# The last part of a two-part transformer kernel: its last 256 features in two groups, the closing norm's factor by feature on ScalarE, the store by two k-tiles, and other places of tiles in SBUF

## The chip, the cores and the metric

The kernel runs on one NeuronCore of a Trainium2 chip. The metric is the time of one execution on the device in microseconds. The change is measured against the kernel before, in runs on one chip.

## The reference, cut to what matters

256 tokens of 1024 features go through two models, one behind the other, each two layers deep. The first has a context of 256 tokens beside them in its first layer; the second is called `second_block` here. All of it is fp32.

```python
def first_block(x, c, ctx, ...):
    for l in range(2):
        # h = modulate(rms_norm(x)), the same for ctx; local and grouped attention, merged with gates
        x = x + g1 * branch_merge(ya, yb, ga, gb, w_pa[l], w_pb[l], w_o[l])
        # ctx likewise where l is 0
        h2 = modulate(rms_norm(x, norm2[l]), sh2, sc2)
        x = x + g2 * swiglu(h2, w_ffn_in[l], w_ffn_out[l])
    return rms_norm(x, final_norm)

def swiglu_2(h, w_gu, w_down):                      # w_gu: 1024 x 5632, w_down: 2816 x 1024
    g, u = jnp.split(h @ w_gu, 2, axis=-1)
    return (jax.nn.silu(g) * u) @ w_down

def second_block(x, ...):
    for l in range(2):
        x = x + 0.5 * swiglu_2(rmsnorm(x, g_ffn1[l]), w_ffn1_gu[l], w_ffn1_down[l])
        x = x + hybrid_mixer(rmsnorm(x, g_mix[l]), w_in[l], ...)
        x = x + 0.5 * swiglu_2(rmsnorm(x, g_ffn2[l]), w_ffn2_gu[l], w_ffn2_down[l])
    return rmsnorm(x, g_final)                      # x / sqrt(mean(x*x) + eps) * g_final
```

## The kernel before

Features lie on the 128 partitions, tokens along the free dimension: `x` is 128 x 8 x 256, and a "k-tile" is 128 features of it. Every matmul that counts is done as three: an fp32 operand is split into a high part, rounded to TensorE's fp32r, and a low part, the rest. For a weight, `Weights.next` loads raw pieces of up to 128 x 1024 by SP (`wf_1r` and the like), and for each 128 x 512 of them ScalarE writes the high half (`hw*`, L403) and VectorE the low half (`lw*`, L408, raw minus high); eight buffers of each go round. `group` (L427 issues its matmuls) takes for each k the pairs high weight with high input, high weight with low input and low weight with high input. The weight is the stationary operand, 128 x 128; the input is the moving one, 256 tokens wide, or 512 in layer 0 of the first part, where the context goes along.

The inputs' names: `hh`, `hl` are the high and low part of a normed x in the first part (`inputs_of`, 8 k-tiles, each 516 columns wide, so that neighbouring k-tiles lie 2064 bytes apart); `gh`, `gl` the same in the second part; `acth`, `actl` the gated activations of a feed-forward; `yh`, `mh` and their `l` those of attention and of the mixer's merge. `wb` are weights of the first part's layers, `wf` those of a feed-forward (ffn2) and `wmx` of a mixer in the second part.

The tiles' places in SBUF follow from the pools' order and the tiles' sizes. In the built program, within a partition and modulo 256 bytes: raw, high and low weights 128; `gh`, `gl` and `x` 224; `act`, `yh`, `mh`, `sg`, `rt` 0; `hh` and `hl` 32 + 16k and 160 + 16k in layer 0, 0 + 16k and 128 + 16k in layer 1's feed-forward, for k-tile k.

The order on each engine is set by a scheduler that lists instructions by a modelled time, with some held back by hand: `MIX_HOLD` is the number of low weight halves that may go ahead of a mixer's last `gl` on VectorE (`L408 gl<-hn`, the low part of the mixer's normed input), and `HOLD` does the like for the row factors.

A feed-forward of the second part, `ffn2`, has 22 groups of gate/up, and then `add_x` for the down projection, four groups of 256 features with 22 k-tiles each, i.e. 132 matmuls of 256 columns. After a group, VectorE multiplies the two 128-feature halves of the result by the row factor of the norm ahead of it (`rt`, L1258) and adds that to x (L1262); ScalarE squares it (L478), VectorE adds the squares' two halves (L483), TensorE transposes them (L486) and VectorE reduces over the features into a column of `sums` (L488). After the last group, `rstd_rows` makes the row factor: mean (L504 to L509), an integer start and three Newton steps (L522 to L536), two transposes that spread it over the partitions (L542), a copy to SBUF on ScalarE (L550, `rsb`). `store` multiplies each k-tile by the feature's factor `gfin` and by that row factor (L1767, eight times 128 x 256), and SP stores four k-tiles at a time (L1771).

## Time and profile before

| what | value |
|---|---|
| time, median of 3 runs (lowest to highest) | 2473.17 us (2472.64 to 2473.49) |
| the profiled execution's own time | 2474.45 us |
| its span | 2472.6 us |
| TensorE busy | 2404.3 us (97%) |
| VectorE, ScalarE busy | 1821.5 us (74%), 1357.2 us (55%) |
| mean granted clock of TensorE | 0.988 |

The span is the time between the first and the last instruction of that execution; its own time also has what lies around. Busy times are per engine and overlap. Matmuls are pipelined: the length that the trace gives for one reaches into the next, so what one costs is read from start to start, or from the length of a piece of the chain of waits and the number of matmuls in it.

### The profile page before, as it was taken

Reading aid. Unit: us, or ns where it says so; the run is one execution under the profiler, and the core shown is the slowest. Engines: PE = TensorE matmul, PEld = TensorE weight load, DVE = VectorE, ACT = ScalarE, POOL = GpSimd, SP = SyncE. Lnnn points to the kernel's source line nnn. Section 1 sums busy time; section 2 is a strip of 40 time slices with the busy share of each in tenths; the row PEclk is TensorE's granted clock in tenths of the full one; section 3 lists DMA queues with packets and bytes.
Section 4 is the critical chain, followed back from the end, with each engine's and each line's share of the span. In section 5 each row is a group of like instructions: output and inputs, shape, how many; then the busy total and the mean of one; then the engine's idle time right before and its main releaser. Section 6 shows DMA issues by size and latency. Waiting matters only on the chain.

```text
span 2472.6 us, 45747 instructions
## 1 busy us (share of the span) xinstructions
PE 2404.3 (97%) x17232; PEld 2243.4 (91%) x17232; DVE 1821.5 (74%) x4115; ACT 1357.2 (55%) x2666; POOL 0.2 (0%) x4
## 2 busy tenths in 40 slices
PE   7999999999999999999999999999999999999997
PEld 4877779888888898999999998999999999899997
DVE  5777667885766888776676688886666669888665
ACT  4566544322223676665555567765555556776553
POOL 0000000000000000000000000000000000000000
PEclk9999999999999999999999999999999999899999
DMA  7221462553653333465555553455555555345553
GB/s 276 85 73 52 160 232 95 171 188 131 218 184 119 129 112 115 146 187 183 184 182 181 182 183 117 138 173 184 177 186 187 178 184 183 106 135 188 180 179 103
DMA packets 112542, 393.45 MB, mean 159 GB/s; under 512 B 12480, under 2 KB 13760, under 8 KB 111808
## 3 DMA queue, kind: packets, MB, share of 16 engines
q1 hardware_dynamic: 112320, 390.52, 48.8%
q8 instruction: 136, 2.23, 0.4%
q14 instruction: 86, 0.70, 0.1%
HBM read 389.42 MB, written 1.05 MB: 158 GB/s over the span
## 4 chain that ended last, share of the span: by engine, by line
PE 91%; DVE 5%; ACT 2%; issue 1%; DMA 1%; SPq 0%; DVEq 0%; ACTq 0%
PE mm L427 82%; PE y L427 2%; PE s L427 1%; PE s L798 1%; PE mm L616 1%; PE y L805 1%; DVE lwmx L408 1%; PE s L751 1%; PE y L486 0%; DMA wm0r<-in_wm_dram 0%; DVE kl L408 0%; ACT pt L775 0%; ACT hwmx L403 0%; PE y L682 0%; DVE ptl L408 0%
## 5 line engine op out<-in xcount | busy, mean ns | idle before, releaser
L427 PE MATMUL mm<-hh,hwb 128*128 128x512 f32 (+2 forms) x1176 | 349.1, 341 | 3.1 <-ACT gt L1027 1.6
L427 PE MATMUL mm<-hl,hwb 128*128 128x512 f32 (+1 forms) x1176 | 350.0, 340 | 0.2 <-DVE hl L408 0.2
L427 PE MATMUL mm<-hh,lwb 128*128 128x512 f32 (+2 forms) x1176 | 346.7, 340 | 0.0
L403 ACT ACTIVATE hwb<-wb_0r 128x512 fp32r<-128x512 f32 (+1 forms) x250 | 149.9, 612 | 261.4 <-PE mm L427 242.4
L427 PE MATMUL mm<-gh,hwf 128*128 128x256 f32 x1344 | 272.1, 283 | 0.0
L427 PE MATMUL mm<-gh,lwf 128*128 128x256 f32 x1344 | 270.7, 282 | 0.0
L427 PE MATMUL mm<-gl,hwf 128*128 128x256 f32 x1344 | 270.6, 282 | 0.0
L408 DVE TENSOR_TENSOR lwf<-wf_1r,hwf 128x512 fp32r<-128x512 f32 (+1 forms) x272 | 183.8, 676 | 110.2 <-ACT hwf L403 103.9
L408 DVE TENSOR_TENSOR lwf<-wf_0r,hwf 128x512 fp32r<-128x512 f32 (+1 forms) x272 | 183.6, 676 | 103.4 <-ACT hwf L403 96.7
L403 ACT ACTIVATE hwf<-wf_1r 128x512 fp32r<-128x512 f32 (+1 forms) x272 | 168.2, 619 | 166.6 <-PE mm L427 153.7
L403 ACT ACTIVATE hwf<-wf_0r 128x512 fp32r<-128x512 f32 (+1 forms) x272 | 168.2, 619 | 165.3 <-PE mm L427 149.4
L427 PEld LDWEIGHTS mm<-hh,hwb 128*128 128x128 f32 x1176 | 203.7, 189 | 30.3 <-ACT gt L1027 2.7
L408 DVE TENSOR_TENSOR lwb<-wb_0r,hwb 128x512 fp32r<-128x512 f32 (+1 forms) x250 | 163.6, 666 | 89.5 <-ACT hwb L403 85.5
L427 PEld LDWEIGHTS mm<-hl,hwb 128*128 128x128 f32 x1176 | 204.5, 189 | 25.8 <-DVE hl L408 0.8
L427 PEld LDWEIGHTS mm<-hh,lwb 128*128 128x128 f32 x1176 | 203.9, 189 | 25.4
L403 ACT ACTIVATE hwb<-wb_1r 128x512 fp32r<-128x512 f32 (+1 forms) x242 | 146.6, 612 | 117.6 <-PE mm L427 107.3
L427 PEld LDWEIGHTS mm<-gh,hwf 128*128 128x128 f32 x1344 | 207.5, 189 | 0.0
L427 PEld LDWEIGHTS mm<-gh,lwf 128*128 128x128 f32 x1344 | 206.7, 188 | 0.0
L408 DVE TENSOR_TENSOR lwb<-wb_1r,hwb 128x512 fp32r<-128x512 f32 (+1 forms) x242 | 158.5, 667 | 65.2 <-ACT hwb L403 62.5
L427 PEld LDWEIGHTS mm<-gl,hwf 128*128 128x128 f32 x1344 | 205.8, 188 | 0.0
L427 PE MATMUL mm<-gh,hwmx 128*128 128x256 f32 x656 | 140.5, 288 | 4.6 <-DVE kl L408 2.1
L427 PE MATMUL mm<-actl,hwf 128*128 128x256 f32 x704 | 142.0, 283 | 0.0
(393 smaller groups left out, 5558.8 us busy)
## 6 DMA issues: line engine op xcount, KB each, us to landing
wf_0r<-in_wf_dram SPq DMA_DIRECT2D x120, 512.0 KB, 3.5
wf_1r<-in_wf_dram SPq DMA_DIRECT2D x120, 512.0 KB, 3.6
wb_0r<-in_wb_dram SPq DMA_DIRECT2D x108, 512.0 KB, 3.8
wb_1r<-in_wb_dram SPq DMA_DIRECT2D x105, 512.0 KB, 3.7
wmx_0r<-in_wmx_dram SPq DMA_DIRECT2D x49, 512.0 KB, 3.6
wmx_1r<-in_wmx_dram SPq DMA_DIRECT2D x49, 512.0 KB, 3.6
wm2r<-in_wm_dram SPq DMA_DIRECT2D x48, 512.0 KB, 3.6
wm1r<-in_wm_dram SPq DMA_DIRECT2D x24, 512.0 KB, 4.7
```

What stands on the lines that cost most here:

```text
L403: self.nc.scalar.activation(out, src, AF.Copy, scale=scale)
L408: return self.nc.vector.tensor_tensor(out, src, h, ALU.subtract)
L427: i = nc.tensor.matmul(out, lhsT, rhs, start=bank not in first, stop=n[bank] == 0, skip_group_check=True)
L616: nc.tensor.matmul(ps[32 * j : 32 * j + 32], self.scp[:, k], t[:, o : o + 512], start=k < 4, stop=k >= 4, skip_group_check=True,)
L751: nc.tensor.matmul(out, q, part, start=n == 0, stop=n == 1, skip_group_check=True)
L798: nc.tensor.matmul(s[:, :nk], q[:, o], part, start=n == 0, stop=n == 1, skip_group_check=True)
L805: nc.tensor.transpose(tp[:, j * P : (j + 1) * P], pt[:, j * P : (j + 1) * P], self.ident)
```

## The change

The last feed-forward of the second part (`wf2_1`) gets its last 256 features as two groups of 128. For this `add_x` is replaced there by `last_x`: five groups (three of two k-tiles, two of one), and for a single k-tile a new `square_sum` that squares 256 columns and transposes these, with no halves to add. `sums` has five columns there. `last_x` also lets ScalarE multiply x by `gfin`, one k-tile at a time and in place, right behind its squares. `store` then has only the row factor left: four products of two k-tiles each, and a store behind each.

Elsewhere: `MIX_HOLD` goes from 5 to 6. `inputs_of` makes k-tiles 512 columns wide (520 for layer 1's feed-forward), and `qg`, `four` and `one` become wider tiles of which the same columns are used. In the built program the weights' tiles then lie at 160 modulo 256 bytes, and `act`, `yh`, `mh`, `sg`, `rt` and layer 0's `hh` and `hl` at 224, where `gh`, `gl` and `x` stay; layer 1's feed-forward has `hh` and `hl` at 224 + 32k. The number of matmuls and of raw loads is the same.

```diff
--- before.py
+++ after.py
@@ -109,9 +109,12 @@
 GQ_ROWS = [r for i in range(4) for h in (i, 4 + i) for r in _r(HD * h, HD)]
 
 
-def spec_ffn2(gu, down):
+def spec_ffn2(gu, down, last=False):
     s = [(gu, _r(128 * m, 128) + _r(DFF + 128 * m, 128), (8,)) for m in range(22)]
-    return s + [(down, _r(256 * j, 256), KP_DOWN) for j in range(4)]
+    cols = [_r(256 * j, 256) for j in range(4)]
+    if last:
+        cols[3:] = _r(768, 128), _r(896, 128)
+    return s + [(down, c, KP_DOWN) for c in cols]
 
 
 QA, KA, VA, FA, QB, KB, VB, QC, CKV, QI, KI, WI, GT = (
@@ -133,7 +136,7 @@
 
 
 
-MIX_HOLD = 5
+MIX_HOLD = 6
 MIX_ORDER = (
     "K S0 G8 T0 T1 F0 s0 S2 s1 S1 G1 G9 s3 G10 F1 s2 s4 x0 B3 G5 x2 G4 x1 d1 F2 x3 d0 G2 G0 G11 x4 x5 d2 d3 B1 G7 G3 d4 d5 A0 B2".split()
 )
@@ -188,7 +191,7 @@
     SPECS[f"wb1_{_l}"] = (_l, spec_b1(_l))
     SPECS[f"wf1_{_l}"] = (_l, spec_ffn2("w_ffn1_gu_2", "w_ffn1_down_2"))
     SPECS[f"wmx_{_l}"] = (_l, spec_mix())
-    SPECS[f"wf2_{_l}"] = (_l, spec_ffn2("w_ffn2_gu_2", "w_ffn2_down_2"))
+    SPECS[f"wf2_{_l}"] = (_l, spec_ffn2("w_ffn2_gu_2", "w_ffn2_down_2", _l == 1))
 
 
 def pieces(n, kparts):
@@ -487,6 +491,16 @@
         self.hold(0, i, hold)
         nc.vector.tensor_reduce(ss[:, j], ps[:, :SEQ].rearrange("p (t f) -> p t f", t=2), AX.X, ALU.add)
 
+    def square_sum(self, x, ss, m, j, pool):
+
+        nc = self.nc
+        sq = pool.tile([P, 2, SEQ], F32, tag="sq", name=self.u("sq"), bufs=2)[:, 0]
+        nc.scalar.activation(sq, x[:, m], AF.Square)
+        ps = self.bank("y")
+        for t in range(2):
+            nc.tensor.transpose(ps[:, t * P : (t + 1) * P], sq[:, t * P : (t + 1) * P], self.ident)
+        nc.vector.tensor_reduce(ss[:, j], ps[:, :SEQ].rearrange("p (t f) -> p t f", t=2), AX.X, ALU.add)
+
     def sums(self):
         return self.small(8, tag="sums").rearrange("p (j t) -> p j t", j=4)
 
@@ -500,8 +514,8 @@
         nc = self.nc
         p, v = self.small(2), self.small(2)
         t = ss.rearrange("p j t -> p t j")
-        if last == 3:
-            nc.vector.tensor_reduce(p, t[:, :, :3], AX.X, ALU.add)
+        if last >= 3:
+            nc.vector.tensor_reduce(p, t[:, :, :last], AX.X, ALU.add)
         else:
             nc.vector.tensor_reduce(p, t[:, :, 2:], AX.X, ALU.add)
             nc.vector.tensor_tensor(p, p, ss[:, 0], ALU.add)
@@ -576,9 +590,9 @@
             self.hi(hh[:, k : k + 2, c], t)
             self.last_norm = self.lo(hl[:, k : k + 2, c], t, hh[:, k : k + 2, c])
 
-    def inputs_of(self, pool):
-
-        return [pool.tile([P, NKT, 516], F32R, tag=f"h{c}", name=self.u(f"h{c}")) for c in "hl"]
+    def inputs_of(self, pool, n=2 * SEQ):
+
+        return [pool.tile([P, NKT, n], F32R, tag=f"h{c}", name=self.u(f"h{c}")) for c in "hl"]
 
 
     def setup_mod(self):
@@ -599,7 +613,7 @@
         self.scp = pool.tile([P, NKT, 32], F32, name="scp")
         nc.vector.memset(self.scp, 0.0)
         nc.vector.tensor_copy(self.scp[:, :, :2], self.sc)
-        self.four = pool.tile([P, 2], F32, name="four")
+        self.four = pool.tile([P, 64], F32, name="four")[:, :2]
         nc.vector.tensor_tensor(self.four, self.ident[:, 0:2], self.ident[:, 32:34], ALU.add)
         for j in (64, 96):
             nc.vector.tensor_tensor(self.four, self.four, self.ident[:, j : j + 2], ALU.add)
@@ -848,7 +862,7 @@
                         m = self.b1_merge(1, w, y[0], gates, mr.enter_context(self.open("mr1", "right")), T)
                 self.tc.keep_in_program_order(nc.scalar.preload_act_table_set("silu_and_others"))
                 self.amplitude(l, 1, len(self.xs))
-                h = self.inputs_of(hn)
+                h = self.inputs_of(hn, 520 if l else 2 * SEQ)
                 self.residual(
                     l, w, range(NKT), m, T, 16, hn, lambda i: self.norm_mod(l, 1, i, self.xs[i], h, hn, self.rsb[i]),
                     early=(lambda k: self.unnormed(l, k, h)) if l else None, place="ac"[l],
@@ -956,7 +970,7 @@
         full = lambda k: (hh[:, k, :512], hl[:, k, :512])
         mine = lambda k: (hh[:, k, :T], hl[:, k, :T])
         nt = T // P
-        qg = self.small(1, tag="qg", bufs=1)
+        qg = self.sp.tile([P, 64], F32, tag="qg", name=self.u("qg"), bufs=1)[:, :1]
         nc.vector.tensor_scalar(qg, self.p(f"qg{l}"), HD**-0.5, None, ALU.mult)
         bias_tile = lambda: ap.tile([P, 2, SEQ], F32, tag="bias", name=self.u("bias"), bufs=2)
         rot = bias_tile()
@@ -1265,6 +1279,32 @@
                 self.gained(gain, self.x, range(2 * j, 2 * j + 2))
         self.rsb = [self.rstd_rows(ss, hold=hold)]
 
+    def last_x(self, w, ks, xs, pool, rsb, scale):
+
+
+        nc = self.nc
+        ss = self.small(10, tag="sums").rearrange("p (j t) -> p j t", j=5)
+        for j, (m, n) in enumerate(((0, 2), (2, 2), (4, 2), (6, 1), (7, 1))):
+            if n == 2:
+                _, (b,) = self.pair(w.next(), ks, xs, SEQ)
+            else:
+                b = self.bank("mm")
+                self.group([(0, b[:, :SEQ], 0, P, None)], w.next(), ks, xs)
+            t = pool.tile([P, 2, SEQ], F32, tag="rt", name=self.u("rt"), bufs=2)[:, :n]
+            xv = self.x[:, m : m + n]
+            nc.vector.scalar_tensor_tensor(
+                t, b[:, : n * SEQ].rearrange("p (k t) -> p k t", k=n), scale,
+                rsb.unsqueeze(1).broadcast_to((P, n, SEQ)), ALU.mult, ALU.mult,
+            )
+            nc.vector.tensor_tensor(xv, xv, t, ALU.add)
+            if n == 2:
+                self.square_sums(self.x, ss, j, pool)
+            else:
+                self.square_sum(self.x, ss, m, j, pool)
+            for k in range(m, m + n):
+                nc.scalar.activation(self.x[:, k], self.x[:, k], AF.Copy, scale=self.p("gfin", k, 1))
+        self.rsb = [self.rstd_rows(ss, 4)]
+
     def ffn2(self, name, gain, late=None):
         nc = self.nc
         w = Weights(self, name)
@@ -1285,7 +1325,10 @@
                 acts += [(h[:, j], lo[:, j]) for j in range(2)]
                 if late and m > 2:
                     next(late, None)
-            self.add_x(w, range(22), lambda k: acts[k], fp, rsb, 0.5, gain, name[:3])
+            if gain is None:
+                self.last_x(w, range(22), lambda k: acts[k], fp, rsb, 0.5)
+            else:
+                self.add_x(w, range(22), lambda k: acts[k], fp, rsb, 0.5, gain, name[:3])
         assert w.off == w.ap.shape[0] and w.i == len(w.spec)
 
     def mixer(self, l):
@@ -1758,17 +1801,15 @@
             self.rsb = [self.rstd_rows(ss)]
 
     def setup2(self):
-        self.one = self.cp.tile([P, 1], F32, name="one")
+        self.one = self.cp.tile([P, 9], F32, name="one")[:, :1]
         self.nc.vector.memset(self.one, 1.0)
 
     def store(self, out):
         nc = self.nc
-        for k in range(NKT):
-            nc.vector.scalar_tensor_tensor(
-                self.x[:, k], self.x[:, k], self.p("gfin", k, 1), self.rsb[0], ALU.mult, ALU.mult
-            )
-            if k % 4 == 3:
-                nc.sync.dma_start(out[:, k - 3 : k + 1], self.x[:, k - 3 : k + 1])
+        for k in range(0, NKT, 2):
+            xv = self.x[:, k : k + 2]
+            nc.vector.tensor_tensor(xv, xv, self.rsb[0].unsqueeze(1).broadcast_to((P, 2, SEQ)), ALU.mult)
+            nc.sync.dma_start(out[:, k : k + 2], xv)
 
 
 def program(tc, ins, out, stages=("b10", "b11", "b20", "b21", "end"), dump=None):
```

What the scheduler makes of it, at two places. In a mixer (layer 1's is shown; `lwmx_7_2` is the low half of a weight for the values' projection, `vs` are scaled values, `hn` the normed input), VectorE has before:

```order
L408 TENSOR_TENSOR lwmx_7_0_17068<-wmx_0r_17065,hwmx_7_0_17067 128x512
L408 TENSOR_TENSOR gl_15786<-hn_16901,gh_15785 128x512
L409 SCALAR_TENSOR_TENSOR vs_16699<-mm_16835,rcol_16417,vs_16699 128x5x64
L409 SCALAR_TENSOR_TENSOR vs_16699<-mm_16836,rcol_16417,vs_16699 128x5x64
L408 TENSOR_TENSOR gl_15786<-hn_16906,gh_15785 128x512
L408 TENSOR_TENSOR lwmx_7_2_17072<-wmx_0r_17065,hwmx_7_2_17071 128x512
L408 TENSOR_TENSOR lwmx_7_4_17078<-wmx_0r_17075,hwmx_7_4_17077 128x512
L408 TENSOR_TENSOR lwmx_7_6_17082<-wmx_0r_17075,hwmx_7_6_17081 128x512
```

and now:

```order
L412 TENSOR_TENSOR lwmx_7_0_17068<-wmx_0r_17065,hwmx_7_0_17067 128x512
L412 TENSOR_TENSOR gl_15786<-hn_16901,gh_15785 128x512
L412 TENSOR_TENSOR lwmx_7_2_17072<-wmx_0r_17065,hwmx_7_2_17071 128x512
L413 SCALAR_TENSOR_TENSOR vs_16699<-mm_16835,rcol_16417,vs_16699 128x5x64
L413 SCALAR_TENSOR_TENSOR vs_16699<-mm_16836,rcol_16417,vs_16699 128x5x64
L412 TENSOR_TENSOR gl_15786<-hn_16906,gh_15785 128x512
L412 TENSOR_TENSOR lwmx_7_4_17078<-wmx_0r_17075,hwmx_7_4_17077 128x512
L412 TENSOR_TENSOR lwmx_7_6_17082<-wmx_0r_17075,hwmx_7_6_17081 128x512
```

`lwmx_7_2` has moved from behind the last `gl<-hn` to ahead of the two `vs` and of that `gl`. On TensorE the order moves too: in both mixers, and at the end of layer 1's attention in the first part, where transposes of `pt` and score matmuls stand earlier than before.

At the end of the program, VectorE has before (from the last group's scaling on):

```order
L504 TENSOR_REDUCE small_30677<-sums_29864 128x2
L508 TENSOR_SCALAR small_30677<-small_30677 128x2
L1258 SCALAR_TENSOR_TENSOR rt_30667<-mm_30534,rsb_28218 128x512
L1262 TENSOR_TENSOR x_3790<-x_3790,rt_30667 128x512
L483 TENSOR_TENSOR sq_30670<-sq_30670 128x256
L488 TENSOR_REDUCE sums_29864<-y_30673 128x2
L509 SCALAR_TENSOR_TENSOR small_30678<-sums_29864,small_30677 128x2
L522 TENSOR_SCALAR rcol_30682<-small_30678 128x2
```

and now (from the first 128-feature group's scaling on):

```order
L1295 SCALAR_TENSOR_TENSOR rt_30577<-mm_30480,rsb_28218 128x256
L1299 TENSOR_TENSOR x_3790<-x_3790,rt_30577 128x256
L502 TENSOR_REDUCE sums_29864<-y_30582 128x2
L518 TENSOR_REDUCE small_30694<-sums_29864 128x2
L522 TENSOR_SCALAR small_30694<-small_30694 128x2
L1295 SCALAR_TENSOR_TENSOR rt_30684<-mm_30587,rsb_28218 128x256
L1299 TENSOR_TENSOR x_3790<-x_3790,rt_30684 128x256
L502 TENSOR_REDUCE sums_29864<-y_30689 128x2
L523 SCALAR_TENSOR_TENSOR small_30695<-sums_29864,small_30694 128x2
L536 TENSOR_SCALAR rcol_30699<-small_30695 128x2
```

The addition of the squares' halves (L483 before) is gone for these groups, and the one scaling, addition and reduction of the last group have become two of half the width.

ScalarE has at the same place before:

```order
L403 ACTIVATE hwf_1_26_17_30520<-wf_1r_30514 128x512
L403 ACTIVATE hwf_1_26_19_30526<-wf_1r_30524 128x512
L403 ACTIVATE hwf_1_26_21_30530<-wf_1r_30524 128x256
L478 ACTIVATE sq_30670<-x_3790 128x512
L550 COPY rsb_30702<-y_30699 128x256
```

and now:

```order
L407 ACTIVATE hwf_1_27_19_30614<-wf_1r_30608 128x384
L498 ACTIVATE sq_30580<-x_3790 128x256
L1305 ACTIVATE x_3790<-x_3790,par 128x256
L498 ACTIVATE sq_30687<-x_3790 128x256
L1305 ACTIVATE x_3790<-x_3790,par 128x256
L564 COPY rsb_30719<-y_30716 128x256
```

The products with `gfin` (L1305) now stand behind each square.

## Rows read from the trace of the kernel before

**Rows 1.** The page: busy time and its share by engine; then the chain's shares.

```profile
PE 2404.3 (97%) x17232; PEld 2243.4 (91%) x17232; DVE 1821.5 (74%) x4115; ACT 1357.2 (55%) x2666; POOL 0.2 (0%) x4
...
PE 91%; DVE 5%; ACT 2%; issue 1%; DMA 1%; SPq 0%; DVEq 0%; ACTq 0%
```

**Rows 2.** Groups by shape: count, then total busy us, mean ns, idle before.

```profile
L427 PE MATMUL mm<-gh,hwf 128*128 128x256 f32 x1344 | 272.1, 283 | 0.0
...
L427 PE MATMUL mm<-hh,hwb 128*128 128x512 f32 x592 | 228.9, 398 | 1.6 <-ACT hh L403 0.9 <-ACT gt L1027 0.7
...
L408 DVE TENSOR_TENSOR lwf<-wf_1r,hwf 128x512 fp32r<-128x512 f32 x256 | 177.1, 692 | 105.7 <-ACT hwf L403 99.4 <-PE mm L427 2.9
...
L427 PE MATMUL mm<-actl,hwf 128*128 128x256 f32 x704 | 142.0, 283 | 0.0
...
L427 PE MATMUL mm<-gh,hwmx 128*128 128x256 f32 x656 | 140.5, 288 | 4.6 <-DVE kl L408 2.1 <-ACT fw L1395 1.7 <-DVE gate L1548 0.8
...
L427 PE MATMUL mm<-acth,hwb 128*128 128x256 f32 x260 | 53.2, 285 | 0.0
```

**Rows 3.** The chain in four stretches: start us, length us, line and count.

```profile
1079.96 100.04 PE mm L427 x848
...
2289.99 100.08 PE mm L427 x834
...
2417.41 15.67 PE mm L427 x132
...
534.81 56.94 PE mm L427 x245
```

**Rows 4.** Windows: busy us (instructions) of PE, PEld, DVE, ACT, POOL; PEclk, DMA.

```profile
2290.00:2390.00 100.00, 100.00 (x835) 100.00 (x835) 66.45 (x114) 55.75 (x96) 0.00 (x0) 1.00 0.58 184
1520.00:1530.00 10.00, 6.45 (x42) 5.77 (x40) 9.79 (x32) 6.64 (x15) 0.00 (x0) 0.88 0.35 112
1530.00:1540.00 10.00, 9.24 (x50) 8.68 (x49) 9.01 (x25) 6.87 (x17) 0.00 (x0) 0.60 0.01 2
```

**Rows 5.** Timeline of PE at 1103 us: start us, length us, operation, count.

```profile
1103.16 0.39 PE L427 MATMUL mm<-hl,hwb 128*128 128x256 f32 x2
1103.39 0.40 PE L427 MATMUL mm<-hh,lwb 128*128 128x256 f32 x2
...
1103.86 0.41 PE L427 MATMUL mm<-hl,hwb 128*128 128x256 f32 x2
1104.10 0.40 PE L427 MATMUL mm<-hh,lwb 128*128 128x256 f32 x2
```

**Rows 6.** The chain behind the last matmul.

```profile
2458.95 0.70 DVE rt L1258
...
2459.68 0.70 DVE x L1262
...
2460.40 0.64 ACT sq L478
...
2461.06 0.44 DVE sq L483
```

**Rows 7.** Timeline of DVE at 24.71 us, and of all engines at the end.

```profile
24.71 2.49 DVE L1743 TENSOR_TENSOR xin<-xin,rsb 128x512 f32<-128x512 f32 x4
...
2465.18 0.37 ACT L550 COPY rsb<-y 128x256 f32<-128x256 f32 x1 [4.15 <-PE y L542]
2465.59 3.25 DVE L1767 SCALAR_TENSOR_TENSOR x<-x,par,rsb 128x256 f32<-128x256 f32 x8 [1.12 <-ACT rsb L550]
```

**Rows 8.** By line and tile: count, then min, median and max ns.

```profile
L1281 DVE TENSOR_TENSOR sg<-mm,rsb x84: 413/425/427, 1255.1 to 2395.6; 128x256 f32<-128x256 f32 x84
...
L482 ACT ACTIVATE sq<-x,par x8: 492/498/501, 1191.8 to 1240.5; 128x256 f32<-128x256 f32 x8
```

**Rows 9.** The store's line: issue in ns, and time from issue to landing.

```profile
L1771 SPq DMA_DIRECT2D out_dram<-x x2: 344/346/348, 2467.3 to 2468.9; - x2
...
DMA to landing us min/median/max: 2.6/2.6/2.6
```

**Rows 10.** Timeline of PE in layer 0's mixer, idle time before and its releaser.

```profile
1525.78 0.56 PE L1689 MATMUL s<-ph,stickr 128*128 128x256 f32 x3 [2.57 <-ACT ph L403]
```

## The prediction

> **What bounds the kernel now.** I read the page first: TensorE is busy 97% of the span and the chain that ended last runs through it for 91% [rows 1]. So a microsecond is saved either where TensorE streams without a gap, by making one matmul shorter, or at the very end, where it has nothing left to do. The groups of matmuls come next [rows 2]. Each product of fp32 operands is three matmuls (high by high, high by low, low by high), and the reader is to see the counts: 1344 for each of the three products on gh and gl in the second part's gate/up, 656 in its mixers, 704 on act in its down projections, 592 of 512 columns on hh and hl in the first part's layer 0. The mean durations there (283 to 398 ns) overlap; the pitch, start to start, is what counts, and the chain gives it as a piece's length by its count.
>
> Four such pieces [rows 3], without a gap in them (the second also as a window: TensorE busy for all of 100 us at full clock [rows 4]): 100.04 us for 848, or 117.97 ns each, for the first part's feed-forward in layer 1; 100.08 us for 834, or 120.0 ns, for the last feed-forward's gate/up; 15.67 us for 132, or 118.7 ns, for its down projection; and 56.94 us for 245 of 512 columns, or 232.4 ns. The first three do the same work: 128x128 stationary, 256 columns moving, no waits. They differ by where their tiles lie in a partition, modulo 256 bytes. Stationary tiles (hw, lw) lie at 128 everywhere. The moving ones lie at 224 (gh, gl: 96 above), at 0 (act, 128 above), and in layer 1's hh and hl at a place that steps by 16 bytes with each k, so all sixteen differences come up, once for each of the 8 k on hl (0 to 112) and twice on hh (128 to 240, since hh meets hw and lw). That stage's mean is 117.97. The differences 96 and 128, taken alone, cost 120.0 and 118.7, both above that mean; so others must lie below it. In one feature group of that stage, the two hl matmuls of k=4 (difference 64) begin at 1103.16 and the next pair at 1103.39: 0.23 us; those of k=5 (80) take from 1103.86 to 1104.10: 0.24 [rows 5]. That is 115 against 120 ns, each read to 5 ns at worst, the same sign as the argument from the means.
>
> **The change, part by part.**
> *Places.* `inputs_of` loses its 4 pad columns, `qg` and `four` get 64 wide, `one` 9 wide. In the built programs the stationary tiles move to 160 and nearly all moving ones (act, mh, yh, layer 0's hh and hl) to 224, where gh and gl already were: the difference becomes 64. Layer 1's feed-forward steps by 32 bytes, and I leave it at its mean, nothing gained or lost. No run of before has a whole stage at 64, so its cost is bounded: below by the 115 ns of the pair, above by what the same tiles cost today. I take 116.5, halfway between that 115 and the mean of 117.97, since the pair is read coarsely but the means demand something below 117.97.
> - gh, gl: 3 x (1344 + 656) = 6000 [rows 2] x (120.0 - 116.5 = 3.5 ns) = 21.0 us.
> - act, 3 x (704 + 260) = 2892, in the second part's down projections and in the first part's of layer 1 [rows 2], both at place 0: x (118.7 - 116.5 = 2.2 ns) = 6.4 us. Smaller groups at that place (mh, yh) I leave out.
> - 512 columns: 3 x 592 = 1776. They go through all steps of 16 now, so only the gain from mean to best counts, and per matmul I take it as in the 256-column case: 1.5 ns, 232.4 to 230.9. 1776 x 1.5 = 2.7 us.
> Together 30.1 us. What stands outside full streams gives nothing back; TensorE carries 91% of the chain as a whole and all of it in the stages named, except the mixers, so I keep 0.95 of it: 28.6. Bounds: at 115 ns for all, 6000 x 5 + 2892 x 3.7 + 1776 x 3 = 46.0 us, at 0.95 43.7; at 117.5, 6000 x 2.5 + 2892 x 1.2 + 1776 x 0.5 = 19.4, or 18.4; the other side is in the rivals below.
>
> *The end.* Today, after the last matmul, the chain is [rows 6]: scale by the row factor 0.70, add 0.70, square on ScalarE 0.64, the two halves added 0.44, two transposes, reduction, mean and Newton steps, two transposes of the factor, a copy, then the eight products of the store. Afterwards the last group has 128 features, so these are 256 wide instead of 512. From 256-wide rows of the same kind [rows 8]: a product with the row factor 0.425 (-0.27), the add, taken like it (0.42, -0.27), the square 0.50 (-0.14); the halves' add and its step go (-0.46). The reduction, the 1-column Newton steps and the factor's transposes stay. The store's 3.25 us for eight products [rows 7] become four plain products 128x512: four on the same engine, with the factor broadcast, took 2.49 [rows 7]: -0.76. The last DMA carries 256 KB instead of the 512 that land in 2.6 us [rows 9]: half of it cannot give more than 1.3, and SP issues two more, each of them beside a product of the store; I take -0.3, bounds -1.3 to +0.3. Added: one more pair of square transposes, each of 128 columns, in TensorE's queue; two matmuls of 256 columns bound it with 0.24. It stands behind the second to last group's products, and its square (0.43 + 0.42 + 0.50 us after the group) is ready under the last group's 66 x 0.118 = 7.8 us of matmuls; if it were waited for, 1.4 us. Sum: -0.27 -0.27 -0.14 -0.46 -0.76 -0.3 +0.24 = -2.0; bounds -3.0 to -0.5.
> The factors by feature move to ScalarE: eight products of 256 columns, each like a square of 256 at 0.50 [rows 8], 4.0 us. Six stand among the weights' high halves, which ScalarE makes in 55% of its time (1357.2 us) [rows 1], with eight buffers between them and TensorE; the seventh and the eighth stand between a square and the factor's copy. The eighth hides in the 4.15 us that ScalarE idles before that copy [rows 7]; without that cover it would cost 0.50. The weights' traffic is the same: as many raw loads, halves and matmuls, in pieces 384 and 512 wide.
>
> *Orders.* MIX_HOLD at 6 lets one more low half of a weight go ahead of the scaled inputs' last `gl` in the mixers (lwmx_7_2 now ahead of two vs rows and that gl); TensorE's order shifts at layer 1's attention and in the mixers too. `lwmx_7_2` is 0.69 us of VectorE [rows 2], so the vs rows and that gl come so much later, and the weight half so much earlier. TensorE does idle in the mixers: it is busy 6.45 of 10 us at 1520, and then gets 0.60 of its clock for 10 us, the lower level of 1.2 GHz in most of it [rows 4]. But the longest of that idling, 2.57 us, stands ahead of `s<-ph`, a later step, and not at the rows that move [rows 10]. I take 0, bounds -5 and +5: what one stretch like this costs (3.6 idle and about 4 at half clock) could be lost or saved in part.
>
> Sum: -28.6 - 2.0 + 0 = -30.6. The profiled execution took 2474.45 us, its span 2472.6 and 1.85 around it; it is 1.28 above the median of 2473.17. A difference carries over: 2474.45 - 30.6 = 2443.9 for an execution like it, 2442.6 against the median.
>
> **The rivals.**
> *The best place is no better than the mean.* The pair of rows 5 is a reading of two hundredths; if difference 64 costs 118.0, places give (6000 x 2.0 + 2892 x 0.7) x 0.95 = 13.3, the end 2.0: 2458. For it: the stepping stage's mean is itself near 118. Against: two of its parts alone lie above it. Chance 0.18.
> *Places give nothing*, and what differs among the three stages is something else about them, such as which tiles were written last. Then the end alone remains: 2471, within 0.2%. For it: only three stages carry the argument. Against: the two uniform stages follow each other in one feed-forward, with the same weights' path and TensorE full in both. Chance 0.08. The Trainium skill, page "TensorE: Matmul & The Clock Gate", section "Step-by-step: what each phase is for", says that TensorE has two independent read ports, one for the moving operand and one for weights, so that loading weights takes nothing from the running matmul. By that rule places are worth nothing and the time would be 2471; the 117.97, 118.7 and 120.0 ns for equal matmuls speak against it, though no row shows why they differ.
> *It is the moving tile's own place that costs.* gh and gl are the dearest of the three stages and the only ones wholly at 224; the change brings all others there. Then gh and gl stay at 120.0 (stationary tiles don't matter), and 2892 x 1.3 = 3.8 us are lost on act; the 512-column ones would go from 232.4 in the ratio 120.0/117.97 to 236.4, 1776 x 4.0 = 7.1. 10.9 x 0.95 = 10.4 less 2.0: +8.4, 2482. It decides where the pitch at 224 stays above 119.3: below that, what 6000 on gh and gl win outweighs the rest. For it: the three means don't exclude it. Against: act at 0 and the stepping stage, which meets 0 and 224 among its places, differ by 0.7 ns only. Chance 0.08.
>
> **How the numbers follow.** The forecast (a pitch from 115 to 117.5 at 64) has 0.66, and its own range is 2428 to 2453 (-43.7 and -18.4, and the end's 2.0). The rival of 2458 with the orders' 5 above it takes the range to 2464. Left out are those of 2471 and 2482, and the ends of the orders' bounds: about 0.19. Two runs of this kernel can be told apart from 0.2% on, 4.9 us: faster is 0.66 + 0.18 = 0.84, the same 0.08, slower 0.08.
>
> **What would show it.** In the profile after: the pitch of the last gate/up and of its down projection by the chain's pieces, 116 to 117 for both where right, 120 where the third rival holds, 118 for the first; the three products by gh equally many in each. The tail from the last matmul's end to the factor's copy 1.1 us shorter and the store's products at 2.5. In the mixers, the windows of the half clock as long as now. The prediction is wrong if the pitches stay where they are, or if the half clock spreads to new stretches.

## The result and the profile after

The changed kernel took 2441.72 us (median of 4 runs, 2440.5 to 2442.93), the kernel before beside it 2472.9 us (2472.12 to 2473.49). The ratio is 0.9874 with a 95% interval of 0.9857 to 0.9891: 31 us less, 1.3%. The prediction was 2442.6. The profiled execution has a span of 2440.0 us, 32.6 under that of before.

The page after, as [rows 1] of before: busy time by engine and the chain's shares.

```profile
PE 2372.8 (97%) x17234; PEld 2218.2 (91%) x17234; DVE 1819.4 (75%) x4113; ACT 1360.4 (56%) x2675; POOL 0.2 (0%) x4
...
PE 91%; DVE 5%; ACT 2%; issue 1%; DMA 1%; SPq 0%; DVEq 0%; ACTq 0%
```

TensorE is busy 31.6 us less with two matmuls more (17234 against 17232, the added pair of transposes), and the chain looks as it did. So what is gone is time inside TensorE's stream. The chain's pieces that answer to [rows 3] (start us, length us, line and count; line 427 is 431 now):

```profile
1079.98 80.09 PE mm L431 x680
...
2259.90 100.11 PE mm L431 x850
...
2387.44 14.60 PE mm L431 x124
...
531.21 56.10 PE mm L431 x245
```

The first is layer 1's feed-forward of the first part: 80.09 / 680 = 117.78 ns a matmul, 117.97 before. The last gate/up: 100.11 / 850 = 117.78, 120.0 before. Its down projection: 14.60 / 124 = 117.7, 118.7 before. 512 columns: 56.10 / 245 = 229.0, 232.4 before.

The end, as [rows 6] and the last two of [rows 7] and [rows 9]; first the chain behind the last matmul, then the timeline, then the store's time from issue to landing:

```profile
2428.76 0.44 DVE rt L1295
...
2429.22 0.44 DVE x L1299
...
2429.73 0.42 ACT sq L498
...
2430.20 0.45 PE y L501 x2
```

```profile
2430.18 0.51 ACT L1305 ACTIVATE x<-x,par 128x256 f32<-128x256 f32 x1
...
2433.78 0.37 ACT L564 COPY rsb<-y 128x256 f32<-128x256 f32 x1 [3.09 <-PE y L556]
2434.18 2.50 DVE L1811 TENSOR_TENSOR x<-x,rsb 128x512 f32<-128x512 f32 x4 [1.12 <-ACT rsb L564]
```

```profile
DMA to landing us min/median/max: 2.1/2.2/2.3
```

From the first operation behind the last matmul (2428.76, before 2458.95) to the end of the span it is 11.24 us, before 13.65: 2.4 less. The reader sees each part: scaling and addition 0.44 each instead of 0.70, the square 0.42 instead of 0.64, no row for the halves' addition, 2.50 for the store's products instead of 3.25. The last product with `gfin` (0.51) lies at 2430.18, beside the transposes, and the copy of the row factor still finds ScalarE idle for 3.09 us.

Where the 32.6 us came from, stage by stage, by when the first matmul of the stage's first weight starts in both traces (each entry is rounded, so that they add up to 0.2 more):

| stage | gained, us |
|---|---|
| first part, layer 0 | 7.1 |
| first part, layer 1, up to its feed-forward | 3.2 |
| its feed-forward | 1.1 |
| second part, ffn1 and ffn2 of layer 0 | 3.5 and 2.8 |
| ffn1 and ffn2 of layer 1, up to the last matmul | 3.4 and 2.7 |
| mixers of layer 0 and 1 | 2.8 and 3.8 |
| the end | 2.4 |

### The profile page after: what moved, and what is told of

Its sections match the earlier page's. It is cut to its first block, busy times and chain, and to the rows that moved or that the text cites. A ratio compares the mean times of both kernels' runs of the same rounds, so it can differ in the third digit from the quotient of the medians.

```text
span 2440.0 us, 45755 instructions
## 1 busy us (share of the span) xinstructions
PE 2372.8 (97%) x17234; PEld 2218.2 (91%) x17234; DVE 1819.4 (75%) x4113; ACT 1360.4 (56%) x2675; POOL 0.2 (0%) x4
## 4 chain that ended last, share of the span: by engine, by line
PE 91%; DVE 5%; ACT 2%; issue 1%; DMA 1%; SPq 0%; DVEq 0%; ACTq 0%
PE mm L431 82%; PE y L431 2%; PE s L431 1%; PE s L812 1%; PE y L819 1%; PE mm L630 1%; DVE lwmx L412 1%; PE s L765 1%; DVE kl L412 1%; PE y L490 0%; DMA wm0r<-in_wm_dram 0%; ACT hwmx L407 0%; PE y L696 0%; ACT pt L789 0%; PE y L556 0%
## 5 line engine op out<-in xcount | busy, mean ns | idle before, releaser
L412 DVE TENSOR_TENSOR lwf<-wf_1r,hwf 128x512 fp32r<-128x512 f32 (+2 forms) x272 | 183.6, 676 | 105.5 <-ACT hwf L407 92.9
L407 ACT ACTIVATE hwf<-wf_1r 128x512 fp32r<-128x512 f32 (+2 forms) x272 | 168.1, 619 | 158.0 <-PE mm L431 145.9
L431 PE MATMUL mm<-acth,hwf 128*128 128x256 f32 x704 | 143.3, 279 | 0.0
```

The lines of the kernel that those rows point to most:

```text
L407: self.nc.scalar.activation(out, src, AF.Copy, scale=scale)
L412: return self.nc.vector.tensor_tensor(out, src, h, ALU.subtract)
L431: i = nc.tensor.matmul(out, lhsT, rhs, start=bank not in first, stop=n[bank] == 0, skip_group_check=True)
```

## The experiments

My theory after the result: a matmul's pitch follows the difference between the places of the moving and the stationary tile, modulo 256 bytes; 64 is better than 96 and 128. Rivals: one of the two places by itself does it; or it is the order of the instructions that gained. Four kernels take the change apart, and the others sweep the places.

**e1: the places alone.** The kernel before with

```diff
-        self.one = self.cp.tile([P, 1], F32, name="one")
+        self.one = self.cp.tile([P, 9], F32, name="one")[:, :1]
-        self.four = pool.tile([P, 2], F32, name="four")
+        self.four = pool.tile([P, 64], F32, name="four")[:, :2]
-        qg = self.small(1, tag="qg", bufs=1)
+        qg = self.sp.tile([P, 64], F32, tag="qg", name=self.u("qg"), bufs=1)[:, :1]
-    def inputs_of(self, pool):                          # 516 columns
+    def inputs_of(self, pool, n=2 * SEQ):               # n columns
-                h = self.inputs_of(hn)
+                h = self.inputs_of(hn, 520 if l else 2 * SEQ)
```

> The kernel before with the wider tiles alone (one, qg, four, and inputs_of at 512 and 520 columns): stationary tiles at 160, nearly all moving ones at 224, old end, MIX_HOLD 5. If the matmul's pitch follows the difference of the two places (my theory): gate/up and down at 117.8 ns as in the changed kernel, 512 columns at 229.0, and about 2473 less 25 to 29, 2444 to 2448. If half of the gain came from the orders in the mixers that MIX_HOLD moves: 2455 or more.

Measured: 2459.82 us against 2472.63, ratio 0.9952 (0.9939 to 0.9964). That is 12.8 us less, not half of the change's gain, and in the second case's range. But the pitch came as the first had it. The chain's pieces in the last gate/up, its down projection and the 512 columns:

```profile
2274.96 100.11 PE mm L427 x850
...
2402.97 15.55 PE mm L427 x132
...
529.17 56.10 PE mm L427 x245
```

That is 117.78, 117.80 and 229.0 ns, as in the changed kernel. By the stages' starts e1 had gained as much as the changed kernel up to the first mixer (within 2 us), and then lost 8.4 us between the mixer's weight groups 23 and 30, and 8.8 us at the same place in the other mixer. The windows there (us; busy us and count of PE, PEld, DVE, ACT, POOL; granted clock; DMA share and GB/s) and one of the waits from 1584 to 1600 (total us, times, longest):

```profile
1585.00:1590.00 5.00, 3.96 (x32) 3.54 (x31) 4.96 (x18) 3.56 (x11) 0.00 (x0) 1.00 0.35 100
1590.00:1595.00 5.00, 4.07 (x30) 3.41 (x30) 4.15 (x20) 2.88 (x10) 0.00 (x0) 1.00 0.31 98
1595.00:1600.00 5.00, 3.51 (x16) 2.94 (x17) 4.32 (x20) 3.69 (x13) 0.00 (x0) 0.78 0.11 42
```

```profile
PE y L427 <- ACT ph L403: 2.4, 3, 1.0
```

TensorE is busy 3.96, 4.07 and 3.51 of 5 us, VectorE nearly throughout in the first; the chain there goes through VectorE's `s`, `lwmx` and `gate` and ScalarE's `pt`. Then the granted clock falls to 0.78, part of that time at 1.2 GHz. Nobody touched the mixer in e1: with the places, the scheduler found another order for it.

**e2: only the tiles on the left side of SBUF moved.** As e1, without the line on `one`: stationary tiles stay at 128, `gh` and `gl` 96 above; `act`, `mh`, `yh`, layer 0's `hh` and `hl` come to 192, which is 64 above.

> The kernel before with inputs_of, qg and four as in the change, but one left as it was: stationary tiles stay at 128, gh and gl at 224 (difference 96), act, mh, yh and layer 0's hh and hl at 192 (difference 64, another place than 224). By the difference: gate/up of the second part stays at 120.0 ns, its down projection falls from 118.7 to 117.7, 512 columns fall from 232.4 to 229.0; the end of layer 1's attention, whose order moves with inputs_of, gives its 3 us here too; 2473 less 7 (layer 0), 3 (that order), 3 (act): 2460. If the stationary's own place 160 is what helps: down at 118.7, 512 at 232.4, 2470. If 224 is what helps the moving ones: the same, 2470.

Measured: 2477.28 us (median of ten, 2472.69 to 2478.45), ratio 1.0015 (1.0006 to 1.0025): neither of the two times. The pitches decide all the same; the chain in the last gate/up, its down projection and the 512 columns:

```profile
2286.79 98.27 PE mm L427 x819
...
2421.36 15.55 PE mm L427 x132
...
530.86 56.10 PE mm L427 x245
```

120.0, 117.8 and 229.0 ns: only what came to 64 improved, and it did so at 192 over 128 as at 224 over 160. So neither 160 for the weights nor 224 for the inputs is needed. By the stages' starts in the profiled execution, the longest of the ten, layer 0 gained 7.4 us, layer 1's attention 2.9; and the two mixers lost 8.7 and 9.0 us at the place where e1 lost its 8. e1 and e2 have the same order on every engine. What they have in common is the narrower `inputs_of` and the wider `qg` and `four`, with MIX_HOLD at 5; which of the three moves the order was not tried.

**e3: MIX_HOLD alone.**

```diff
-MIX_HOLD = 5
+MIX_HOLD = 6
```

> The kernel before with MIX_HOLD at 6 alone. The prediction put the moved orders at 0 with 5 either way. The two mixers gained 6.6 us in the changed kernel, of which 1968 matmuls by 2.2 ns explain 4.3: if the rest is MIX_HOLD's, 2471; if it is the places', 2473. Pitch of gate/up 120.0 in both cases.

Measured: 2472.9 us, ratio 1.0 (0.9991 to 1.0009). Alone it does nothing. Its profile tells something else: the end of layer 1's attention is 1.5 us shorter than in the profile of before, with the same order on TensorE there. The windows over the same work, of before, of e3 and of the changed kernel:

```profile
1010.00:1050.00 40.00, 38.92 (x314) 38.72 (x313) 31.06 (x58) 24.03 (x43) 0.00 (x0) 0.96 0.51 152
```

```profile
1008.00:1047.00 39.00, 37.59 (x312) 37.22 (x312) 31.21 (x59) 23.74 (x42) 0.00 (x0) 1.00 0.50 155
```

```profile
1001.00:1040.00 39.00, 37.09 (x315) 36.90 (x314) 32.97 (x64) 25.93 (x47) 0.00 (x0) 1.00 0.53 168
```

In before the clock is 0.96, i.e. one short stretch at 1.2 GHz; in e3 it is 1.00. So of the 3.2 us that the changed kernel gained here, up to 1.5 are that stretch, which can be there or not with the same instructions, and the rest goes with the moved order and the pitch, which no run separates here.

**e4: the end alone.** `last_x`, `square_sum`, the new `mean` and `store` of the changed kernel in the kernel before.

> The kernel before with the new end alone (last_x, square_sum, gfin on ScalarE, stores by two k-tiles), old places and MIX_HOLD 5. By the prediction's sum 2.0 us less, and by the changed kernel's trace 2.4 less between the last matmul and the end: 2470.5 to 2471. If the two groups of 128 or ScalarE's products delay the weights' halves in the last down projection: no gain, 2473.

Measured: 2470.7 us, ratio 0.9993 (0.9985 to 1.0002): 1.9 us less, but the interval includes no change at all. The chain has it more sharply: its last piece of matmuls and the first operation behind it.

```profile
2455.32 0.22 PE y L501 x2
2455.54 3.93 PE mm L431 x33
...
2459.49 0.44 DVE rt L1295
```

From 2459.49 to the end of the span of 2470.7 it is 11.21 us, as in the changed kernel (11.24). The transposes of the second to last group's squares take 0.22 in TensorE's stream, and matmuls follow them at once.

**e5: places and MIX_HOLD 6, old end.**

```diff
 (as e1, and)
-MIX_HOLD = 5
+MIX_HOLD = 6
```

> The kernel before with the places of e1 and MIX_HOLD at 6, old end. In e1 the places gave their pitch (117.8) and then lost 8 us in each mixer between the weights' groups 23 and 30, where the order that the scheduler found with the new places waits for ph and pt; MIX_HOLD 6 alone moved nothing (e3). If MIX_HOLD 6 takes just that loss away: 2459.8 less 16, 2444, and the rest of the changed kernel's gain is the end's 2. If the loss in e1 belongs to the places themselves (operands of the attention in the mixers at another place): still 2459.

Measured: 2444.99 us, ratio 0.9888 (0.9872 to 0.9905): 27.4 less. The first case: MIX_HOLD 6, worth nothing alone, is worth 15 with these places. The windows at the place where e1 lost time:

```profile
1585.00:1590.00 5.00, 5.00 (x47) 5.00 (x46) 5.00 (x20) 3.67 (x11) 0.00 (x0) 1.00 0.54 165
1590.00:1595.00 5.00, 4.18 (x35) 3.84 (x33) 4.79 (x19) 4.09 (x12) 0.00 (x0) 1.00 0.25 84
1595.00:1600.00 5.00, 4.76 (x40) 4.51 (x39) 4.96 (x15) 3.31 (x9) 0.00 (x0) 1.00 0.17 62
```

TensorE is full up to 1590 and busy 4.18 and 4.76 of 5 us in the two windows after that, at full clock, with VectorE full in the first. The two edits cannot be priced apart: the places move the mixers' order for the worse, and MIX_HOLD 6 moves it again, for the better.

**e6 to e11: the sweep.** The changed kernel with the widths of `one` and `qg` alone changed, so that the stationary tiles lie at another place and all moving ones at 224 as before. The order on every engine is the changed kernel's in all six. Each was run once.

```diff
-        self.one = self.cp.tile([P, 9], F32, name="one")[:, :1]
+        self.one = self.cp.tile([P, 41], F32, name="one")[:, :1]       # e10; 17, 25, 57, 33, 49 in e6, e7, e8, e9, e11
-        qg = self.sp.tile([P, 64], F32, tag="qg", name=self.u("qg"), bufs=1)[:, :1]
+        qg = self.sp.tile([P, 32], F32, tag="qg", name=self.u("qg"), bufs=1)[:, :1]   # e10; 56, 48, 16, 40, 24
```

> The changed kernel with the stationary tiles at 192 instead of 160, all moving ones left at 224 (one 17 wide, qg 56): difference 32. If only the differences 96 and 128 are dear and 117.8 is what a matmul costs otherwise: 117.8 again, 2442. If the difference has a best value at 64: between 118 and 119, 2445 to 2455.

> The changed kernel with the stationary tiles at 224 as the moving ones (one 25 wide, qg 48): difference 0. If tiles at the same place got in each other's way: 120 or more, 2460 and more. If only 96 and 128 are dear: 117.8, 2442.

> The changed kernel with the stationary tiles at 96 (one 57 wide, qg 16), moving ones at 224: difference 128, for gh and gl and act alike, with other places of its own than before. If the difference decides: 118.7 in gate/up and down both, as act had it before at 128 and 0; 6000 x 0.9 + 2892 x 0.9 ns = 8 us and some for 512 columns (232.4 or more): about 2455. If a place of its own decides, the two kinds of tiles at 224 need not come out alike with what act at 0 cost.

> The changed kernel with the stationary tiles at 0, moving ones at 224 (one 33 wide, qg 40): difference 224. Measured so far for 256 columns: 0 120.0, 32 116.67, 64 117.78, 96 120.0, 128 118.66 ns; for 512: 226.7, 233.3, 228.9, not measured alone, 233.4. If the size of the difference decides and not its sign, 116.67 and 233.3 as with 32, 2443. If the sign counts, something else; the mean over sixteen differences (117.97 and 232.4) leaves 224, 192 and 160 near 117.3 on average.

> The changed kernel with the stationary tiles at 32, moving ones at 224 (one 41 wide, qg 32): difference 192. If the size alone decides: 117.78 and 228.9 as with 64, 2442. If the sign counts: something else, near 117.3.

> The changed kernel with the stationary tiles at 64, moving ones at 224 (one 49 wide, qg 24): difference 160. If the size alone decides: 120.0 as with 96, 2460 and more. If the sign counts: something else, near 117.3.

The chain's pieces, of each kernel one with 512 columns in layer 0 and one in layer 0's ffn2 with 256; e6, e7 and e8 first:

```profile
544.88 40.13 PE mm L431 x172
...
1680.00 100.10 PE mm L431 x858
```

```profile
544.84 40.13 PE mm L431 x177
...
1679.91 100.20 PE mm L431 x835
```

```profile
544.81 40.37 PE mm L431 x173
...
1679.97 100.03 PE mm L431 x843
```

and e9, e10 and e11:

```profile
544.84 40.37 PE mm L431 x173
...
1679.99 100.11 PE mm L431 x846
```

```profile
544.82 40.37 PE mm L431 x173
...
1679.92 100.11 PE mm L431 x850
```

```profile
544.95 40.06 PE mm L431 x171
...
1679.95 100.15 PE mm L431 x844
```

| kernel | difference | ns at 256 columns | ns at 512 columns | time, us |
|---|---|---|---|---|
| e7 | 0 | 120.0 | 226.7 | 2461.51 |
| e6 | 32 | 116.67 | 233.3 | 2443.08 |
| the change | 64 | 117.78, and 113.4 in places (see e12) | 229.0 | 2441.72 |
| before | 96 | 120.0 | | |
| e8; before's down projection | 128 | 118.66; 118.7 | 233.4 | 2462.88 |
| e11 | 160 | 118.66; 117.3 and 120.0 in ffn1 | 234.2 | 2463.46 |
| e10 | 192 | 117.78, and 113.33 | 233.4 | 2428.26 |
| e9 | 224 | 118.3 | 233.4 | 2461.01 |

e6 missed both of its cases, since 32 is better than 64 for 256 columns and worse for 512; the two cancel in the time. e7 came as the first case had it, e8 as the difference has it in its pitch, 8 us above the time that I had forecast for it. In e9 the sign counts: 118.3 at 224 is not the 116.67 of 32, and it missed the 117.3 too. And 512 columns want another difference (0) than 256.

e11 has no single pitch. Its 118.66 is that of the gate/up in ffn2; in the gate/up of ffn1, of layer 0 and of layer 1, with the same difference, the chain has

```profile
1279.92 40.13 PE mm L431 x342
...
1879.90 40.20 PE mm L431 x335
```

which is 117.3 and 120.0 ns. The 120.0 is what 96 cost too, so e11 doesn't show that the sign counts.

e10 broke the theory as well. Its time is 13.5 us under the changed kernel's, mostly since in ffn1 of both layers the same 256-column matmuls, at the same places modulo 256 and in the same order of operations as in ffn2, run at 113.33 ns; the chain in ffn1 of layer 0 and of layer 1:

```profile
1279.92 40.12 PE mm L431 x354
...
1879.99 40.12 PE mm L431 x354
```

40.12 / 354 = 113.3, against 100.11 / 850 = 117.78 in ffn2 above. By the stages' starts e10 gains on the changed kernel 5.8 us in ffn1 of layer 0, 6.8 in ffn2 of layer 0 and ffn1 of layer 1, 3.8 in the mixers and 1.3 in the last ffn2, and loses 4.4 in the first part, where 512 columns cost 233.4. So which pitches were seen goes with the difference, and something else picks one.

**e12: each width at its best difference.** e10, with layer 0's tiles at 32 as the weights (difference 0) and the moving tiles of 256 columns left at 224 (192). Besides the lines below, `qg` is 16 columns wide where e10 has 32.

```diff
-        return self.sp.tile([P, 16], F32, tag=tag, name=self.u(tag), bufs=bufs)[:, :n]
+        return self.sp.tile([P, 8 if tag == "rcol" else 16], F32, tag=tag, name=self.u(tag), bufs=bufs)[:, :n]
+    def shift(self, pool):                     # first in the pools of ffn2, the mixers, layer 1's feed-forward
+        self.nc.vector.memset(pool.tile([P, 48], F32, tag="shift", name=self.u("shift"))[:, :1], 0.0)
```

> The kernel of e10 (stationary tiles at 32, moving 256-column ones at 224, difference 192) with layer 0's 512-column inputs and activations at 32 (difference 0, which gave 226.7 ns in e7 against 233.4 in e10): for it rcol is made 8 columns wide, and a tile of 48 columns of which one is written goes ahead in the pools of layer 1's feed-forward, of ffn2 and of the mixers. The rest, and every engine's order but those 9 writes, is e10's. If a stage's places decide: 512 columns at 226.7, that is 1776 x 6.6 ns and some on act = 14 us off e10's 2428.3: 2414. In e10 the same places gave 113.3 ns in ffn1 of both layers and 117.8 in ffn2: if a stage's own places set that, the same again; if it hangs on how the stage is entered, some of these stages swap between 113.3 and 117.8, 3.4 us each way, 2407 to 2428.

Measured: 2426.24 us, ratio 0.9814 to before (0.98 to 0.9827): the fastest of all, 15.5 us or 0.6% under the changed kernel, 12 over the 2414 of the first case and within the 2407 to 2428 of the second. The 512 columns came as expected:

```profile
539.89 40.12 PE mm L431 x177
```

40.12 / 177 = 226.7, and by the stages' starts 11.2 us off layer 0. Of that, about 4 were gone again by the end of layer 1, whose 256-column inputs now lie at difference 0 too: they run at 120.0 there (9.84 us for 82 in one piece), as in e7, and at 113.6 in e10 (9.66 for 85). Some 1.6 of the 4 are for the most part the clock's, granted at 0.87 in e12 and at 1.00 in e10 over the same 96 matmuls (12.98 and 11.34 us). 4.7 more went in ffn1 of layer 1, by its pitch. The chain in ffn1 of layer 0, ffn2 of layer 0 and ffn1 of layer 1:

```profile
1279.95 40.12 PE mm L431 x354
...
1689.99 50.06 PE mm L431 x425
...
1879.98 40.04 PE mm L431 x340
```

113.33, 117.79, and 117.77 where e10 had 113.33, with the same places and the same order there. The pitch even changes within a stage. The chain in layer 0's ffn1, at the second and third group of the down projection:

```profile
1365.29 14.99 PE mm L431 x132
1380.28 0.22 PE y L490 x2
1380.50 6.60 PE mm L431 x56
```

132 matmuls in 14.99 us are 113.6 ns; then two transposes of squares go between, and the next 56 take 6.60, 117.9 ns. The changed kernel does this too, at difference 64, in the down projection of layer 1's ffn1:

```profile
1974.45 14.97 PE mm L431 x132
...
1989.64 15.55 PE mm L431 x132
```

That is 113.4 and then 117.8, with two transposes of squares between; two other pieces of the changed kernel, 127 matmuls from 1185.84 and 157 from 1242.53, ran at 113.4 as well. Both groups read the same `act` tiles, and each takes its weights through all eight buffers, so it isn't the operands' places that differ between them. This speaks for the last case of the expectation, that it hangs on how a stage is entered; no run set the entry on purpose.

## Why the prediction was right, and by which steps it was not

**The time** was right, 2442.6 for 2441.72, and that it came so close is luck: the pitch of 256 columns gave less than forecast, and 512 columns and the terms put at nothing gave more.

**The reading of the bound** held: the pitch of equal matmuls differed by where their tiles lie, no wait stands in the changed stretches, and e2 shows that it takes only a change of place. The Trainium skill, page "TensorE: Matmul & The Clock Gate", section "Step-by-step: what each phase is for", has two independent read ports and weight loads that take nothing from the running matmul. By that, places would be worth nothing; the runs have 113.33 to 120.0 ns for equal matmuls. That it is the weight loads which take something from the running matmul, no run shows.

**The pitch at 64** was mis-sized. I took 116.5 from a pair of rows read to hundredths; 256 columns came to 117.78, just outside the 115 to 117.5 of the forecast and 0.2 below the first rival's 118.0. So 6000 matmuls on `gh` and `gl` gave 13.3 us and not 21.0, act 2.7 and not 6.4. What failed is the step from the parts of the stepping stage to a whole stage: the pair at difference 64 sat among matmuls at other places, and e10 and e12 show that a matmul's pitch isn't its own. Nor did the reading single out 64: in the same view of before the pair of k=3, at difference 48, takes 0.23 us as well.

```profile
1102.45 0.39 PE L427 MATMUL mm<-hl,hwb 128*128 128x256 f32 x2
1102.68 0.40 PE L427 MATMUL mm<-hh,lwb 128*128 128x256 f32 x2
```

**The 512 columns** were mis-sized the other way: 3.4 ns each instead of 1.5, 6.0 us instead of 2.7. Together 22 us in place of 30.1. By the stages' table the pitch gave about 25: 20.6 outside the mixers and the attention, and 1968 x 2.2 ns = 4.3 of the mixers' 6.6. The smaller groups that I had left out (`mh`, `yh`, `acth` of 512 columns) are in it, and so are the three pieces at 113.4, 416 matmuls by 4.4 ns or 1.8 us. The factor of 0.95 wasn't needed.

**The orders**, 0 with 5 either way, were wrong in the working, though not by much in the sum. What the table leaves for them is 3.2 us at layer 1's attention (up to 1.5 of it the clock) and 2.3 in the mixers: 5.5, just beyond the bound. These are remainders, and how much of them is order and how much pitch or clock isn't shown; but with the end they make up what the pitch didn't give. The granted clock over the two mixers stayed as it was, 0.98 and 0.97 before, 0.98 in both after. And the term hid two of 15: I had compared the order before with the order after, which shows the net of both edits. e1 and e5 show that the places make the mixers' order worse by 15 us and MIX_HOLD 6 takes that back. My sentence that the idling stood elsewhere was right for before, and says nothing of what MIX_HOLD was needed for.

**The end** was right: 2.0 forecast; 2.4 in the trace behind the last matmul, less the 0.22 of the added transposes ahead of it; 1.9 by e4's medians. The scaling, addition and square came within 0.1, the store's products as their row said (2.50 for 2.49). The smaller last DMA lands in 2.1 to 2.3 us instead of 2.6, -0.3 to -0.5 for the -0.3 assumed. ScalarE's products with `gfin` were hidden, as argued.

**The rivals:** "no better than the mean" was right on the pitch of 256 columns and wrong on the time. "Places give nothing" falls with e2, and the moving tile's own place falls with e7 and e8, where 224 costs 120.0 and 118.66.

**Left open:** what picks one of the pitches. At differences 64 and 192 they were 113.33 and 117.78, at 160 117.3, 118.66 and 120.0, at 32 116.67 and in one group 117.9, steady over a hundred matmuls and more, and the pitch could change across a pair of transposes. I take it that weight loads and moving reads fall into a repeating pattern, but that is argued and not shown; no run set the pattern on purpose. The starts of single matmuls go with it: in before's last gate/up they lie 122.9 and 117.1 ns apart by turns (means over 100 us), in the changed kernel's 117 to 119 throughout, so 120.0 is the mean of two unlike steps. Open too is whether places count modulo 256 bytes or modulo a multiple of it: no run moved a tile by 256 bytes alone.

## What to carry to other kernels

Where TensorE is full, divide the length of a stretch without waits by its matmuls, in every stage and not in one for all, since e11 had three pitches in three stages. If equal matmuls differ, try other places for their tiles (here modulo 256 bytes), which costs a few unused columns, and try them for each width apart. An edit that should only move addresses can move a scheduler's order: look at the stages that it isn't meant for, and run each edit alone and all together, since here one that was worth nothing alone was worth 15 us beside the other. A pitch read from a few matmuls among others isn't that of a whole stage.

## What the runs showed of the hardware that was not expected

Equal matmuls of 256 columns ran, without any wait, at 113.33, 116.67, 117.3, 117.78, 118.3, 118.66 or 120.0 ns; at 2.4 GHz (granted clock 1.00 in the stretches) 113.33, 116.67 and 120.0 are 272, 280 and 288 clock periods. The Trainium skill, page "TensorE: Matmul & The Clock Gate", section "Wait — 56ns, not 53.3ns?", gives columns by 2.4 GHz and about 2.5 ns more, which would be 109.2 by estimate; no stage here, where each matmul has a weight load of its own (17234 of either), reached it. For 512 columns it was 226.7 to 234.2 ns. At the same places modulo 256 and with the same instructions a stage could run at 113.33 or 117.78 (differences 64 and 192), and change from one to the other behind two transposes.
